# A gated MLP on one core: its three matrix products by one level of Strassen, on fp16 operands, with the layout work moved to DMA

## Chip, core and metric

The kernel runs on one core of a Trainium2 chip; the other cores are idle. The time is that of the device, in microseconds (us), median of several executions. Where stages inside a run are timed, the numbers are those of its one profiled execution. The engines are called PE (matmul; PEld is its weight load), DVE (vector), ACT (scalar), POOL (GpSimd) and SP (sync, which here only issues DMAs). PSUM is the memory that PE adds its results up in; a bank is here one tile of it, 128 x 512 in fp32.

## The reference

```python
# x (8, 1024, 1024), w_gate and w_up (1024, 4096), w_down (4096, 1024), all float32
gate = x @ w_gate
up = x @ w_up
gate = 0.5 * gate * (1 + np.tanh(np.sqrt(2 / np.pi) * (gate + 0.044715 * gate ** 3)))
return ((gate * up) @ w_down).astype(np.float32)
```

There are 8192 tokens. In units of one matmul instruction (128 x 128 stationary, 128 x 512 moving) each of the three products takes 4096, together 12,288.

## The kernel before

It goes through the tokens in 16 passes of 512. In each pass it transposes x on PE, then forms gate and up for 128 columns at a time, then the down product. The casts of the weights to bf16 are made in the first pass by ACT and DVE; gate and up weights are written back in bf16 and read again in each later pass.

```python
for mi in range(n_mt):                       # 16 passes of 512 tokens
    # [cut: load x, cast to bf16]
    for kc in range(KC):
        tp = tpsum_pool.tile([P, MT], BF16, tag="tps")
        for mm in range(MT // P):
            nc.tensor.transpose(tp[:, mm * P:(mm + 1) * P],
                                xbs[mm][:, kc * P:(kc + 1) * P], identity)
        nc.any.tensor_copy(out=xT_sb[:, kc, :], in_=tp)
    for nb in range(n_nb):
        if mi == 0:
            wg_f = wstage_pool.tile([P, KC, NB], FP32, tag="wsf")
            nc.sync.dma_start(out=wg_f, in_=wg_v[:, :, nsl])
            wg_b = wbf_pool.tile([P, KC, NB], BF16, tag="wgb")
            nc.any.tensor_copy(out=wg_b, in_=wg_f)
            nc.sync.dma_start(out=wg_bf[:, :, nsl], in_=wg_b)
            # [cut: the same for w_up]
        else:
            # [cut: load wg_b and wu_b from the bf16 copies]
        for ns in range(n_ns):
            # [cut: pg, pu = PSUM tiles; 8 matmuls into each]
            nc.scalar.activation(gl, pg, mybir.ActivationFunctionType.Gelu_apprx_tanh)
            nc.vector.tensor_tensor(hT_sb[:, ncidx, :], gl, pu, mybir.AluOpType.mult)
    for m128 in range(n_m128):
        for hh in range(n_hh):
            # [cut: po = PSUM tile; 32 matmuls hT_sb x wd_b into it, copy, store]
```

## Time and profile before

| | before |
|---|---|
| time, median | 2801.5 us |
| matmuls of 512 columns | 12,288 |
| PE transposes | 512 |
| one pass of 512 tokens, from the second on | 168.53 us |
| end of the first pass | 268.5 us |

The page of the kernel before, its first two parts: busy time and share by engine, then the granted PE clock, the DMA engines' busy share (both in tenths) and the GB/s in 40 slices of the span.

```profile
...
PE 2720.0 (97%) x12800; PEld 1234.7 (44%) x12800; DVE 395.4 (14%) x583; ACT 536.0 (19%) x803; POOL 0.7 (0%) x6
...
PEclk9899999999999999999999999999999999999999
DMA  9996534525254352534525254351534525244250
GB/s 342 322 288 204 162 99 140 146 92 154 79 159 126 112 154 73 165 104 136 150 91 150 83 158 128 113 150 65 176 106 135 151 71 155 84 123 133 75 154 35
...
```

PE is busy for 97% of the span. The clock is under 90% in the second slice alone (in stretches of 70 us the windows view has 0.90, 0.85, 0.95, and 1.00 from 210 us on); the DMA engines are at 90% or more of their time in the first three slices.

The chain of waits before, in order of time (start, length, what), from its beginning and around two down phases:

```profile
...
2.94 10.78 DMA x_tile<-in_x_dram
...
59.73 9.50 DMA wg_f<-in_w_gate_dram
69.33 1.91 ACT wg_b L103
...
550.35 55.25 PE po L149 x256
718.88 55.25 PE po L149 x256
...
```

The down phase has 256 matmuls in 55.25 us, so one matmul costs 55.25 / 256 = 0.2158 us of the chain. A pass is 718.88 - 550.35 = 168.53 us: 768 matmuls are 165.7, and 2.8 remain for the transposes. In the first pass the chain goes through weight loads of 4 to 11 us and casts of 1.9 instead.

Groups of instructions before (line, engine, operation, tiles, shapes, count, then busy us, mean ns of one, and idle time before):

```profile
...
L149 PE MATMUL po<-wd_b,hT_sb 128*128 128x512 bf16 x4096 | 891.5, 379 | 6.1 <-DVE hT_sb L141 5.7
...
L141 DVE TENSOR_TENSOR hT_sb<-gl,pu 128x512 bf16<-128x512 bf16 x512 | 352.2, 688 | 1473.1 <-PE pu L130 1457.7
...
```

The mean of 379 ns is the latency of one pipelined matmul, not its cost; the cost is the 0.2158 us above. DVE needs 0.69 us to multiply a bank out of PSUM, and is idle for most of the time.

The whole time is thus 12,288 x 0.2158 = 2652, plus 16 x 2.8 = 45 for transposes, plus 100 lost in the first pass, plus 3.6 of tail: 2800.

### The profile page before, as it was taken

The numbers are of one execution on the slowest core, as the hardware profiler recorded it, in microseconds if no ns is written. First come the engines' busy times: TensorE is split into PE (matmuls) and PEld (weight loads), VectorE is DVE, ScalarE is ACT, GpSimd is POOL, SyncE is SP. The second block draws the span as 40 slices with busy tenths as digits, with TensorE's granted clock in tenths as the row PEclk, the third lists the DMA queues.
The fourth block names the chain that finished last, engine by engine and source line by source line (L and its number), as shares of the span: only waits on it lengthen the run. The fifth ranks groups of instructions, "written<-read, shape, count | busy, mean of one in ns | idle before, by whom it ended". The sixth has DMA issues, their size and how long they took to land.

```text
span 2800.1 us, 29616 instructions
## 1 busy us (share of the span) xinstructions
PE 2720.0 (97%) x12800; PEld 1234.7 (44%) x12800; DVE 395.4 (14%) x583; ACT 536.0 (19%) x803; POOL 0.7 (0%) x6
## 2 busy tenths in 40 slices
PE   5779999999999999999999999999999999999999
PEld 2234444444444444444444444444444444444444
DVE  1111101101021120111101011110211101011010
ACT  4442112111121111112111121111112111121110
POOL 0000000000000000000000000000000000000000
PEclk9899999999999999999999999999999999999999
DMA  9996534525254352534525254351534525244250
GB/s 342 322 288 204 162 99 140 146 92 154 79 159 126 112 154 73 165 104 136 150 91 150 83 158 128 113 150 65 176 106 135 151 71 155 84 123 133 75 154 35
DMA packets 597764, 387.82 MB, mean 139 GB/s; under 512 B 11904, under 2 KB 568960, under 8 KB 597632
## 3 DMA queue, kind: packets, MB, share of 16 engines
q1 hardware_dynamic: 597632, 385.92, 44.9%
q8 instruction: 100, 1.64, 0.2%
q14 instruction: 32, 0.26, 0.0%
HBM read 335.54 MB, written 50.33 MB: 138 GB/s over the span
## 4 chain that ended last, share of the span: by engine, by line
PE 92%; DMA 5%; ACT 1%; issue 1%; SPq 0%; DVE 0%; ACTq 0%; DVEq 0%
PE po L149 31%; PE pg L122 30%; PE pu L130 30%; DMA wg_f<-in_w_gate_dram 3%; DMA wu_f<-in_w_up_dram 1%; PE tp L89 1%; ACT wg_b L103 1%; DMA x_tile<-in_x_dram 0%; ACT wu_b L109 0%; SPq L104 0%; DVE xT_sb L94 0%; ACT wd_b L73 0%; SPq L110 0%; SPq L82 0%; DVE wg_b L103 0%
## 5 line engine op out<-in xcount | busy, mean ns | idle before, releaser
L130 PE MATMUL pu<-xT_sb,wu_b 128*128 128x512 bf16 x4096 | 978.8, 382 | 33.3 <-ACT wu_b L109 33.3
L122 PE MATMUL pg<-xT_sb,wg_b 128*128 128x512 bf16 x4096 | 991.1, 382 | 17.8 <-ACT wg_b L103 16.2
L149 PE MATMUL po<-wd_b,hT_sb 128*128 128x512 bf16 x4096 | 891.5, 379 | 6.1 <-DVE hT_sb L141 5.7
L130 PEld LDWEIGHTS <-wu_b 128*128 128x128 bf16 x4096 | 402.1, 98 | 530.8 <-ACT wu_b L109 40.9
L122 PEld LDWEIGHTS <-wg_b 128*128 128x128 bf16 x4096 | 401.8, 98 | 496.5 <-ACT wg_b L103 19.1
L149 PEld LDWEIGHTS <-hT_sb 128*128 128x128 bf16 x4096 | 399.7, 98 | 492.6 <-DVE hT_sb L141 11.7
L138 ACT ACTIVATE gl<-pg 128x512 bf16<-128x512 f32 x512 | 305.7, 597 | 1369.0 <-PE pg L122 1369.0
L141 DVE TENSOR_TENSOR hT_sb<-gl,pu 128x512 bf16<-128x512 bf16 x512 | 352.2, 688 | 1473.1 <-PE pu L130 1457.7
L157 ACT COPY ot<-po 128x512 f32<-128x512 f32 x127 | 74.5, 586 | 819.4 <-PE po L149 813.1
L94 DVE COPY xT_sb<-tp 128x512 bf16<-128x512 bf16 x33 | 13.8, 422 | 811.5 <-PE tp L89 811.5
L89 PE MATMUL tp<-identity,xb_tile 128*128 128x128 bf16 x512 | 48.6, 223 | 19.2 <-DVE xb_tile L84 12.4
L89 PEld LDWEIGHTS <-xb_tile 128*128 128x128 bf16 x512 | 38.0, 99 | 41.5 <-issue 20.8
L94 ACT COPY xT_sb<-tp 128x512 bf16<-128x512 bf16 x95 | 52.1, 588 | 2.2 <-PE tp L89 2.2
L109 ACT CAST wu_b<-wu_f 128x2048 bf16<-128x2048 f32 x16 | 30.3, 1896 | 15.9 <-DMA wu_f<-in_w_up_dram 15.4
L84 ACT CAST xb_tile<-x_tile 128x1024 bf16<-128x1024 f32 x32 | 32.2, 1047 | 6.1 <-DMA x_tile<-in_x_dram 6.1
L103 ACT CAST wg_b<-wg_f 128x2048 bf16<-128x2048 f32 x14 | 26.6, 1898 | 34.9 <-issue 19.0
L84 DVE CAST xb_tile<-x_tile 128x1024 bf16<-128x1024 f32 x32 | 22.1, 690 | 57.9 <-PE tp L89 40.4
L73 ACT CAST wd_b<-wd_f 128x4096 bf16<-128x4096 f32 x5 | 18.0, 3601 | 13.0 <-DMA wd_f<-in_w_down_dram 13.0
L73 DVE CAST wd_b<-wd_f 128x4096 bf16<-128x4096 f32 x3 | 6.9, 2288 | 0.5 <-DMA wd_f<-in_w_down_dram 0.5
L103 DVE CAST wg_b<-wg_f 128x2048 bf16<-128x2048 f32 x2 | 2.4, 1222 | 3.0 <-DMA wg_f<-in_w_gate_dram 3.0
L73 ACT ACT_TABLE_LOAD x1 | 1.3, 1283 | 0.7 <-PEq L176 0.7
L138 ACT ACT_TABLE_LOAD x1 | 1.3, 1283 | 0.0
(7 smaller groups left out, 1.6 us busy)
## 6 DMA issues: line engine op xcount, KB each, us to landing
wg_b<-geglu_wg_bf SPq DMA_DIRECT2D x240, 512.0 KB, 3.9
wu_b<-geglu_wu_bf SPq DMA_DIRECT2D x240, 512.0 KB, 4.5
x_tile<-in_x_dram SPq DMA_DIRECT2D x64, 512.0 KB, 5.6
out_dram<-ot SPq DMA_DIRECT2D x128, 256.0 KB, 2.0
wd_f<-in_w_down_dram SPq DMA_DIRECT2D x8, 2048.0 KB, 9.5
wg_f<-in_w_gate_dram SPq DMA_DIRECT2D x16, 1024.0 KB, 8.4
wu_f<-in_w_up_dram SPq DMA_DIRECT2D x16, 1024.0 KB, 8.3
geglu_wg_bf<-wg_b SPq DMA_DIRECT2D x16, 512.0 KB, 5.5
```

The costliest lines, as they stand in the source:

```text
L73: nc.any.tensor_copy(out=wd_b[:, c * WDC:(c + 1) * WDC, :], in_=wd_f)
L84: nc.any.tensor_copy(out=xb_tile, in_=x_tile)
L89: nc.tensor.transpose(tp[:, mm * P:(mm + 1) * P], xbs[mm][:, kc * P:(kc + 1) * P], identity,)
L94: nc.any.tensor_copy(out=xT_sb[:, kc, :], in_=tp)
L103: nc.any.tensor_copy(out=wg_b, in_=wg_f)
L109: nc.any.tensor_copy(out=wu_b, in_=wu_f)
L122: nc.tensor.matmul(pg, wg_b[:, kc, ns * P:(ns + 1) * P], xT_sb[:, kc, :], start=(kc == 0), stop=(kc == KC - 1),)
L130: nc.tensor.matmul(pu, wu_b[:, kc, ns * P:(ns + 1) * P], xT_sb[:, kc, :], start=(kc == 0), stop=(kc == KC - 1),)
L138: nc.scalar.activation(gl, pg, mybir.ActivationFunctionType.Gelu_apprx_tanh)
L141: nc.vector.tensor_tensor(hT_sb[:, ncidx, :], gl, pu, mybir.AluOpType.mult)
L149: nc.tensor.matmul(po, hT_sb[:, ncidx, m128 * P:(m128 + 1) * P], wd_b[:, ncidx, hh * HT:(hh + 1) * HT], start=(ncidx == 0), stop=(ncidx == ...
L157: nc.any.tensor_copy(out=ot, in_=po)
```

## The change

One level of Strassen (the form with few additions) replaces a 2 x 2 block product's eight half-size products by seven, at the price of sums of blocks. The change does so for gate, up and down. Other parts come with it:

- 8 passes of 1024 tokens, so that each of x's blocks is 512 x 512;
- fp16 for bf16;
- x is cast by a DMA from DRAM to DRAM and transposed by DMA, for the next pass during the current one, and PE transposes nothing;
- weights are cast by DMA while they are loaded. DVE forms their sums. In passes 0, 1 and half of 2 they come from the fp32 source; raw blocks and sums are stored as "operands" in the second half of pass 1 and the first half of pass 2 and loaded from there afterwards;
- the operands of w_down are prepared in pass 0, through one staging tile: load with cast, four sums on DVE, seven stores;
- a product accumulates onto an earlier one in PSUM; ACT copies a bank out before the next product goes on top, DVE adds other banks, POOL multiplies gelu(gate) by up.

The core of the diff (the removed body is the code above; cuts are marked):

```diff
+    def cast_x(p):
+        r = slice(p * TOK, (p + 1) * TOK)
+        nc.gpsimd.dma_start(out=xh[r, :], in_=x2[r, :])
+    def transpose_x(p):
+        for n, kh, mh in (("b11", 0, 0), ("b21", 1, 0), ("b12", 0, 1), ("b22", 1, 1)):
+            r0 = p * TOK + mh * MH
+            nc.sync.dma_start_transpose(
+                out=xq[n], in_=xh[r0 : r0 + MH, kh * MH : (kh + 1) * MH])
+    def sums_x():                      # [cut: t1..t4, four DVE ops of 128 x 2048 fp16]
+    def load_w(p, i):                  # 2 chunks (gate, up) into a ring of 6
+        # [cut]
+            if from_source(p, i):
+                nc.gpsimd.dma_start(out=raw(c), in_=w_v[w][:, :, i * 2 * P : (i + 1) * 2 * P])
+            else:
+                nc.sync.dma_start(out=c, in_=wop[w][i])
+    def from_source(p, i):
+        return p < 2 or (p == 2 and i < NP // 2)
+    def keeps(p, i):
+        return (p == 1 and i >= NP // 2) or (p == 2 and i < NP // 2)
+    def sums_w(p, i, w):               # [cut: four DVE ops of 128 x 512 fp16]
+        if keeps(p, i):
+            nc.sync.dma_start(out=wop[w][i], in_=c)
+    def wd_load(q):                    # one staging tile, in the first half of hq["s3"]
+        st = hq["s3"].rearrange("p a b -> p (a b)")[:, 0:4096]
+        nc.gpsimd.dma_start(out=st.rearrange("p (t h) -> p t h", t=4),
+                            in_=wd_v[:, 4 * q : 4 * q + 4, :])
+    # [cut: wd_sums(k), four DVE ops of 128 x 1024; wd_store(q), seven stores of 256 KB]
+    SEQ = [("P1", 0), ("P1", 1), ("P5", 0), ("P6", 0), ("P6", 1), ("P5", 1), ("P7", 0),
+           ("P7", 1), ("P2", 0), ("P4", 0), ("P4", 1), ("P2", 1), ("P3", 0), ("P3", 1)]
+    # pair(p, i): per entry of SEQ (0 gate, 1 up) four matmuls; banks a, b, c for each of the two:
+    #   P1, P6, P7, P4 accumulate in a; P5, P3 in b; P2 in c
+        def snap(n, w):
+            nc.scalar.activation(tl((n, w)), bank["a", w], COPY, scale=1.0 if w == 0 else HSC)
+        def add(n, b, w):              # w == 1: the same with a scale of 1/16
+            nc.vector.tensor_tensor(o, bank[b, w], o, ADD)
+        def prod(n, h):
+            nc.gpsimd.tensor_tensor(hq[h][:, i, :], t[n, 1], t[n, 0], MUL)
+    # [cut: h21 on DVE; the table that says after which product each of these is issued]
+    # gate_up(p): for i in range(16), with extra work after the k-th product of a pair:
+            extra[1].append(lambda i=i: load_w(p, i + 2) if i + 2 < NP else None)
+            # [cut: if i + 1 < NP:]
+            extra[3].append(lambda i=i: sums_w(p, i + 1, 0))
+            extra[5].append(lambda i=i: sums_w(p, i + 1, 1))
+            if p == 0:                 # every 21 products: load, and 14 to 17 later sums, stores
+                # [cut]
+            if i == 4 and p + 1 < NPASS:
+                extra[2].append(lambda: cast_x(p + 1))
+    # [cut: down(p): 7 products of 2 x 4 x 8 matmuls; x transposes of the next pass at its start]
+    cast_x(0)
+    load_w(0, 0)
+    load_w(0, 1)
+    transpose_x(0)
+    sums_x()
```

A pair is two of the 32 column tiles of gate and up: 14 products of 4 matmuls, 56 matmuls. The up half is scaled by 1/16 on its way out of PSUM, and the output by 16.

## The prediction

> **What bounds the kernel now.** The page: PE busy 2720 of 2800.1 us (97%), chain 92% PE, 5% DMA. In the chain of waits 256 down matmuls take 55.25 us without a gap, so one 128x128x512 matmul costs 0.2158 us (the 379-382 ns of the groups are latency), and a 512-token pass repeats every 168.53 us: 768 matmuls (165.7) plus 2.8 for transposes. The first pass ends at 268.5, 100 us late: there the chain alternates between weight loads (5 to 11 us per MB) and ACT casts (1.9), at clock 0.92 and DMA 0.93 busy (windows view); the GB/s row peaks at 342. 15 passes then run at the matmul rate, clock 1.00.
>
> **What the change removes and adds.**
> 1. PE: 7/8 of 12,288 matmuls is 10,752 of the same shape, no PE transposes; fp16 should stream like bf16. 10,752 x 0.2158 = 2320 us is the floor.
> 2. Per pair (56 matmuls, 12.1 us): DVE six adds and a multiply from PSUM, 7 x 0.69 (trace: hT_sb) = 4.8; eight weight sums of 512 fp16 in passes 0 to 2.5, an estimated 0.42 each (the Trainium skill, "VectorE: DVE Perf Modes", perf-mode tier table: 16-bit tensor_tensor in SBUF runs at 2x, 1224 ns for 2048; no such case in this trace) = 3.4; sums of w_down in pass 0, 1.8. At most 10 of 12.1. ACT: six copies, four gelus at 0.59 = 5.9. Pool: three products plus descriptors of cast DMAs, guessed 6 to 8 (not in this trace). Copies have 1.7 us before their bank is written again. All hidden, if loads are in time.
> 3. DMA: passes 0 to 2.5 read weights from fp32, 2.1 MB a pair. Pass 0 adds 1.4 MB of w_down reads and 1.2 MB of stores: 4.7 MB per 12.1 us, 390 GB/s, above the 342 seen. Pass 0 loses 20 us (0 to 60), passes 1 and 2, which store operands (347 GB/s), 5 to 15. Later passes need 175 GB/s.
> 4. Start: cast of 4 MB x to DRAM, DMA transposes (2 MB; 261 GB/s in the Trainium skill, "DMA: Bandwidth & Descriptors", Latency and other measured facts; unmeasured here), sums: PE starts at 35 to 45 us. Later transposes hide under down.
> 5. Transitions of 16 phases and tail: 10.
>
> **Sum**: 2320 + 40 + 20 + 10 + 10 = 2400, with unforeseen waits **2410 us, 2365 to 2480** (8 in 10). Faster by over 2%: 0.95; within 2%: 0.03; slower: 0.02.
>
> **What would show it.** Step 1: in passes 3 to 7, 56 matmuls take 12.1 us, a pass (1344) 290 us, PE near 100%, clock 1.00. Step 2: DVE under 85%, ACT near 50% in pass 0; hardly any PE wait on ACT copies or DVE adds. Step 3: 330 GB/s or more in the first tenth of the span, PE waits there released by weight sums that wait on loads; pass 0 at 310 to 350 us, passes 1 and 2 at 290 to 305. Step 4: first matmul at 35 to 45 us, after a transpose or x sums.
>
> **What would make it wrong.** Cast DMAs at half the plain rate, or their descriptors filling Pool: passes 0 to 2.5 bind on loads, plus 50 to 150 us. Pool products blocked by DVE sums. DMA transposes over 40 us each pass, holding up DVE behind the x sums. A clock below 1.00 through short gaps. On the low side: pass 0 hidden and a start under 30 us give 2360.

## The result, and the profile after

The median is 2422.2 us (4 runs, 2417.3 to 2424.3), against 2802.6 for the kernel before in the same rounds. The ratio is 0.8642, 95% interval 0.8628 to 0.8655. The median lies in the predicted range, 12 us over the predicted value. Kernels that ran in different sets are best compared by ratios.

The page after, the same lines as before:

```profile
...
PE 2335.6 (96%) x10752; PEld 1055.0 (44%) x10752; DVE 1027.3 (42%) x1504; ACT 830.1 (34%) x1410; POOL 577.8 (24%) x484
...
PEclk8989999999998999999999999999999999999999
DMA  9999666998797465544756455564645645554453
GB/s 152 180 204 211 177 195 97 175 262 272 170 272 239 174 218 194 204 185 174 225 194 206 177 186 193 215 209 176 206 166 221 210 175 187 210 197 174 175 187 109
...
```

PE is at 96% again. The granted clock is under 90% in slices 1, 3 and 13. The DMA engines, at full share in slices 1 to 4 (up to 242 us), move 152 to 211 GB/s there, where before they moved 288 to 342 in the first three.

The chain of waits after: its start, the ends of passes 0 to 2 (the last of the seven down products), and two loads:

```profile
...
1.25 13.50 DMA x_half<-in_x_dram
16.40 13.43 SPq L91
...
44.62 6.18 DMA x_b<-x_half
...
74.11 14.22 DMA h_s<-in_w_down_dram
...
361.00 13.81 PE ps_da L375 x64
...
651.08 13.81 PE ps_da L375 x64
...
728.41 27.61 DMA wc<-in_w_up_dram
...
954.68 13.81 PE ps_da L375 x64
...
```

A down product is 64 matmuls in 13.81 us, which is again 0.2158 each. Line 91 is the DMA transpose; "SPq" is time in which the sync queue issues it. The last down product ends a pass: 361.00 + 13.81 = 374.8, then 664.9 and 968.5; the next ends come 290.1 apart.

Windows after (per stretch: length, then busy us and count by engine, clock, DMA share, GB/s), for the start, a stretch of pass 0's gate and up, and passes 1, 2 and 3:

```profile
...
core 0: us, PE busy (x) PEld busy (x) DVE busy (x) ACT busy (x) POOL busy (x), PEclk, DMA share, GB/s
0.00:54.80 54.80, 3.59 (x9) 1.13 (x10) 5.10 (x6) 2.48 (x3) 6.94 (x12) 0.84 1.15 167
...
150.00:232.00 82.00, 74.41 (x322) 32.49 (x321) 61.88 (x103) 33.19 (x57) 34.22 (x32) 0.94 1.16 211
...
374.80:664.90 290.10, 290.10 (x1346) 131.48 (x1344) 165.81 (x272) 103.70 (x176) 90.74 (x81) 1.00 0.86 196
664.90:968.50 303.60, 293.13 (x1345) 132.25 (x1344) 128.21 (x192) 103.81 (x176) 72.11 (x60) 0.98 0.72 220
968.50:1258.60 290.10, 290.10 (x1345) 131.48 (x1344) 108.03 (x144) 103.50 (x176) 62.39 (x49) 1.00 0.56 196
...
```

Passes 1 and 3 take 290.1 us, which is 1344 x 55.25 / 256 = 290.06: nothing but matmuls, at full clock. The DMA share adds up the times that packets took; over 1 it says that these times overlap on an engine.

POOL's product in the groups after (L261), and the DMA queues (packets, MB, share of 16 engines' span; q1 plain, q0 the casts issued by POOL):

```profile
...
q1 hardware_dynamic: 142208, 400.59, 46.2%
q0 software_dynamic: 88064, 67.12, 19.1%
...
L261 POOL TENSOR_TENSOR h_a<-t 128x512 f16<-128x512 f32 x384 | 496.7, 1294 | 1510.8 <-DVE t L255 1414.5
...
```

The cast queue has 67.12 MB for 19.1% of the span, which is 67.12 MB / (0.191 x 2422.5 us) = 145 GB/s. The listed size is that of the fp16 result (a weight load of 1 MB of fp32 is listed at 512 KB), so 290 GB/s of fp32 are read. The plain queue has 400.59 MB for 46.2%, or 358 GB/s. These are rates per time that packets took, and since packet times overlap, not what the engines can move: from 14 to 18 us the DMA view shows the cast queue alone, with a share of 1.41 and 187 GB/s of result, or 374 of fp32.

```profile
...
DMA packets 1480, 0.75 MB, mean 187 GB/s; under 512 B 17, under 2 KB 1480, under 8 KB 1480
...
q0 software_dynamic: 1480, 0.75, 140.6%
...
```

Counting a cast by its smaller side is the main reason why a full DMA share shows only some 200 GB/s in pass 0.

Who waited for whom after, between 70 and 260 us (total us, times, longest):

```profile
...
DVE h_s L170 <- DMA h_s<-in_w_down_dram: 31.5, 5, 10.9
POOL h_s L153 <- issue: 22.0, 1, 22.0
...
PE ps_a L241 <- ACT t L248: 12.4, 4, 10.8
...
PE ps_b L241 <- DVE t L253: 9.2, 3, 4.1
...
DVE wc L142 <- DMA wc<-in_w_up_dram: 7.0, 3, 3.8
...
```

The tile h_s is the staging tile of w_down. DVE stands before the w_down sums (line 170), POOL before the w_down loads (153), and PE before banks that ACT and DVE have not yet emptied.

The account of the time, from these numbers:

| term | predicted | measured |
|---|---|---|
| 10,752 matmuls x 0.2158 | 2320 | 8 x 290.06 = 2320.5 |
| start: second product at 54.78 instead of 1.73 us | 40 | 53.0 |
| rest of pass 0: 374.8 - 290.1 - 53.0 | 20 | 31.7 |
| pass 1; pass 2 | 5 to 15 together | 0; 303.6 - 290.1 = 13.5 |
| phase changes, and tail | 10 | 0, and 3.6 |
| sum | 2400, given as 2410 | 2422.3, of a span of 2422.5 |

### The profile page after: what moved, and what is told of

The parts are those of the page before. It is cut to its first block, busy times and chain, and to the rows that moved or that the text cites. A ratio compares the mean times of both kernels' runs of the same rounds, so it can differ in the third digit from the quotient of the medians.

```text
span 2422.5 us, 27727 instructions
## 1 busy us (share of the span) xinstructions
PE 2335.6 (96%) x10752; PEld 1055.0 (44%) x10752; DVE 1027.3 (42%) x1504; ACT 830.1 (34%) x1410; POOL 577.8 (24%) x484
## 3 DMA queue, kind: packets, MB, share of 16 engines
q1 hardware_dynamic: 142208, 400.59, 46.2%
q0 software_dynamic: 88064, 67.12, 19.1%
## 4 chain that ended last, share of the span: by engine, by line
PE 90%; DMA 7%; SPq 1%; DVE 1%; issue 0%; POOL 0%; ACT 0%; POOLq 0%; DVEq 0%; ACTq 0%
PE ps_a L241 33%; PE ps_da L375 18%; PE ps_b L241 17%; PE ps_db L375 9%; PE ps_c L241 8%; PE ps_dc L375 5%; DMA h_s<-in_w_down_dram 3%; DMA wd_ops<-h_s 2%; SPq L91 1%; DMA wc<-in_w_up_dram 1%; DMA x_half<-in_x_dram 1%; DMA x_b<-x_half 0%; SPq L189 0%; DVE t L255 0%; DVE h_s L170 0%
## 5 line engine op out<-in xcount | busy, mean ns | idle before, releaser
L241 PEld LDWEIGHTS <-wc 128*128 128x128 f16 x7168 | 704.3, 98 | 940.6 <-issue 63.3
L261 POOL TENSOR_TENSOR h_a<-t 128x512 f16<-128x512 f32 x384 | 496.7, 1294 | 1510.8 <-DVE t L255 1414.5
L241 PE MATMUL ps_a<-x_t,wc 128*128 128x512 f16 x3072 | 728.3, 380 | 12.4 <-ACT t L248 12.4
L248 ACT ACTIVATE t<-ps_a 128x512 f32<-128x512 f32 x768 | 458.0, 597 | 499.1 <-PE ps_a L241 499.1
L375 PEld LDWEIGHTS <-h_a 128*128 128x128 f16 x3072 | 300.6, 98 | 362.5
L375 PE MATMUL ps_da<-dc,h_a 128*128 128x512 f16 x1536 | 335.4, 379 | 0.0
L241 PE MATMUL ps_b<-x_t,wc 128*128 128x512 f16 x1024 | 264.5, 381 | 21.5 <-DVE wc L142 21.5
L241 PE MATMUL ps_a<-x_b,wc 128*128 128x512 f16 x1024 | 246.8, 385 | 29.8 <-DMA x_b<-x_half 29.8
L241 PE MATMUL ps_b<-x_b,wc 128*128 128x512 f16 x1024 | 246.2, 384 | 19.7 <-DVE t L253 19.7
L241 PE MATMUL ps_c<-x_b,wc 128*128 128x512 f16 x1024 | 262.8, 379 | 0.0
L354 DVE TENSOR_TENSOR h_a<-h_a,h_a 128x2048 f16<-128x2048 f16 x96 | 110.2, 1214 | 0.0
L269 ACT ACTIVATE t<-ps_a 128x512 f32<-128x512 f32 x128 | 76.3, 596 | 65.6 <-PE ps_a L241 65.6
L255 DVE SCALAR_TENSOR_TENSOR t<-ps_c,t 128x512 f32<-128x512 f32 x128 | 88.4, 691 | 11.9
```

What stands on the lines that cost most here:

```text
L241: nc.tensor.matmul(ps, lhs(k), rhs[:, k, :], start=(first and k == 0), stop=(k == KH - 1), skip_group_check=True,)
L248: nc.scalar.activation(tl((n, w)), bank["a", w], COPY, scale=1.0 if w == 0 else HSC)
L255: nc.vector.scalar_tensor_tensor(o, bank[b, w], HSC, o, MUL, ADD)
L261: nc.gpsimd.tensor_tensor(hq[h][:, i, :], t[n, 1], t[n, 0], MUL)
L269: nc.scalar.activation(tl("gl21"), bank["a", 0], GELU)
L354: nc.vector.tensor_tensor(hq[o][:, s, :], hq[a][:, s, :], hq[b][:, s, :], op)
```

## The experiments

Each run edits the kernel after, unless it says otherwise. All had three timed rounds.

### Is the gain the matmul count?

`e_eight` issues P3 twice in each pair and each down phase.

```diff
-            for k in range(KH):
+            for k in list(range(KH)) * (2 if name == "P3" else 1):
-                    for n in range(8):
+                    for n in list(range(8)) * (2 if name == "P3" else 1):
```

> The product P3 is issued twice everywhere (wrong result): 12,288 matmuls again, all else as in the kernel after. Theory (the gain is the matmul count): 1536 more matmuls x 0.2158 = 331 us more, so 2754 us, or down to 2720 where longer pairs hide the loads of the first pass better; 0.97 to 0.985 of before, and a steady pass of 1536 x 0.2158 = 331.5 us. Rival (the gain comes from the new pipeline: cast DMAs, DMA transposes, fp16, buffers): 2450 to 2650.

Measured: 2737.3 us, ratio 0.9775 (0.9761 to 0.979); the result is wrong. A steady pass, in the windows view:

```profile
...
1074.00:1405.50 331.50, 331.50 (x1538) 150.29 (x1536) 108.11 (x144) 103.30 (x176) 62.24 (x49) 1.00 0.51 172
...
```

This is 331.5 us, 1536 x 0.2158, and the total lies in the theory's range. So 315 of the 380 us come from doing seven products for eight. Everything else the change does is worth the remaining 65, or 2.3% of the time before. That 315 is not quite 331 has its place too: in this run pass 0 ended at 401.3, which is 70 over a full pass instead of 85, and pass 2 lost 10 instead of 13.5, presumably because a longer pair hides more of the loads.

`e_bf16` changes only the operand type.

```diff
-FP16 = mybir.dt.float16
+FP16 = mybir.dt.bfloat16
```

> The kernel after with bf16 in place of fp16 everywhere. If the operand type does not matter to the matmul rate or to the sums on DVE: 2415 to 2427 us, steady pass 290.0 to 290.1. If fp16 had cost or gained anything per matmul, a steady pass would differ by more than 1 us. The relative error will be several times that of fp16, it may be judged wrong.

Measured: 2421.4 us, ratio 0.8646 (0.8633 to 0.8659), and correct. The time is that of fp16 within the noise, and in the chain a steady pass runs from 964.35 to 1254.43, again 290.1 us.

### The start

The transposes of pass 0 took the chain from 14.8 to 50.8 us. Over all passes a transpose has a median of 5.3 us to landing. The theory: seven cast DMAs (six for three pairs of weights, one for w_down) run beside the first ones. The rival: a transpose is that slow by itself. `e_start` puts five of the seven (all but the first pair) behind the transposes, by a two-element copy on POOL which reads the last of them:

```diff
     cast_x(0)
     load_w(0, 0)
-    load_w(0, 1)
     transpose_x(0)
+    gate = const.tile([P, 2], FP16, name="gate")
+    nc.gpsimd.tensor_copy(out=gate, in_=xq["b22"][:, 0, 0:2])
+    load_w(0, 1)
@@ gate_up: sums of the second pair, in the first pair of pass 0
-                extra[3].append(lambda i=i: sums_w(p, i + 1, 0))
-                extra[5].append(lambda i=i: sums_w(p, i + 1, 1))
+                late = p == 0 and i == 0
+                extra[11 if late else 3].append(lambda i=i: sums_w(p, i + 1, 0))
+                extra[13 if late else 5].append(lambda i=i: sums_w(p, i + 1, 1))
```

> The second weight pair, the third and the first w_down load are issued only after the four transposes of x have landed (a small Pool copy reads the last one), and the first pair's sums for the second come later in program order. Theory A (the first transposes are slow because seven cast DMAs run beside them): they issue at about 2.5 us each as in later passes, the second product (P5) starts at 30 to 38 us instead of 54.8, total 2398 to 2410 if pass 0 gives little back. Theory B (a transpose of freshly cast x takes 8.5 us of the queue by itself): P5 at 48 or later, total 2418 or more.

Measured: 2403.5 us, ratio 0.8584 (0.8571 to 0.8597), correct. The timelines up to 60 us of the sync queue and of PE (start, us it was taken, what), of the kernel after and of this run:

```profile
...
14.76 33.98 SPq L91 DMA_TRANSPOSE x_b<-x_half  x4
...
54.78 1.89 PE L241 MATMUL ps_b<-x_t,wc 128*128 128x512 f16 x4 [21.45 <-DVE wc L142]
...
```

```profile
...
14.60 11.62 SPq L91 DMA_TRANSPOSE x_b<-x_half  x4
...
32.49 1.89 PE L241 MATMUL ps_b<-x_t,wc 128*128 128x512 f16 x4 [6.62 <-DVE wc L142]
...
```

The same four transposes occupy the queue for 11.62 us instead of 33.98. The second product starts at 32.49 us, 22 earlier, and pass 0 ends at 353.1 instead of 374.8, 22 earlier: in the profiled executions all of it is kept (by the ratios the whole run gained 16 us). Both numbers are in theory A's range, and the rival falls. Why it is kept, though DMA time is short later, is not tested; a likely reason: in the kernel after, the loads issued early soon fill the ring, and from 60 to 68 us the windows view shows no DMA at all, where this run has a share of 1.22.

### The rest of pass 0

The waits above suggest theory A: DVE, in order, stands before the w_down sums until the load has landed. `e_sums_free` lets the sums read x instead, with the same DMA traffic.

```diff
     def wd_sums(k):
-        tt, b11, b12, b21, b22 = wd_views()
+        tt = wd_views()[0]
+        b11 = b12 = xq["b11"][:, 0:2, :]
+        b21 = b22 = xq["b12"][:, 0:2, :]
```

> The w_down sums on DVE read x tiles instead of the just loaded w_down tile (wrong result); the loads and stores of w_down stay, so the DMA traffic is the same. Theory A (in pass 0 DVE, which runs in order, stands before the w_down sums until their load has landed, and the PSUM adds behind them come late): the four PE holes between 70 and 232 us go, DVE no longer waits 31 us for w_down, pass 0 ends at 343 to 352 instead of 374.9, total 2390 to 2402. Theory B (the DMA engines are simply full in pass 0): the wait moves to the weight sums, pass 0 ends at 365 or later, total 2412 to 2424.

Measured: 2416.8 us, ratio 0.8634 (0.8621 to 0.8646), result wrong; pass 0 ended at 368.8. Both numbers lie in theory B's range, and theory A fell as the main cause: only 6 us of 32 came back, 1 of them by an earlier start (by the ratios the whole run gained 2 us, within their intervals). Its waits, 70 to 260 us:

```profile
...
POOL h_s L153 <- DMA wd_ops<-h_s: 34.4, 3, 22.0
...
DVE wc L142 <- DMA wc<-in_w_up_dram: 20.1, 8, 4.8
...
DVE wc L142 <- DMA wc<-in_w_gate_dram: 11.9, 6, 4.2
...
```

DVE no longer waits for w_down, but POOL waits 34 us for the staging tile (in the kernel after 5 us of its waits at line 153 were put down to that, and 22 to nothing that the profile shows), and DVE waits 32 us (20.1 + 11.9) for gate and up weights, where it waited 7. This left theory C, order: POOL stands before the next w_down load until the last stores have read the tile, and weight loads behind it on the same engine start late. Or theory B: the DMA engines are full, and the wait goes wherever it can. `e_wd2buf` separates them. It gives w_down a second staging tile and issues each load but the first 14 products earlier; bytes and sums stay.

```diff
-        st = hq["s3"].rearrange("p a b -> p (a b)")[:, 0:4096]
+        st = st2 if q % 2 else hq["s3"].rearrange("p a b -> p (a b)")[:, 0:4096]
-                        (0, lambda q=q: wd_load(q)),
+                        (0 if q == 0 else -14, lambda q=q: wd_load(q)),
```

(The load stands 28 products ahead of the sums where it stood 14.)

> A second staging tile for w_down, each load issued one period earlier; same bytes, same sums, correct. Theory C (in-order waits: Pool stands before a w_down load until the stores of the last one have read the tile, with weight loads and products behind it; DVE stands before sums until the load lands): waits of Pool and DVE on w_down nearly vanish and pass 0 ends at 352 or earlier, total 2400 or less. Theory B (the DMA engines are full from the start to 232 us, whatever waits for what): waits move to the weight loads, pass 0 ends at 362 to 374, total 2410 to 2422.

Measured: 2421.1 us, ratio 0.8643 (0.863 to 0.8656), correct; pass 0 ended at 373.2. The waits of this run in the same stretch:

```profile
...
DVE wc L144 <- DMA wc<-in_w_gate_dram: 19.7, 5, 8.0
DVE wc L144 <- DMA wc<-in_w_up_dram: 15.2, 7, 4.4
...
```

No wait for the staging tile is left in this view, and nothing was gained: 35 us of waits now stand at the weight loads. Within pass 0 two things nearly cancel: the second w_down load was now issued at 14.8 us, beside the transposes, and the second product started at 57.66, 2.9 later; from there pass 0 lost 27.2 us instead of 31.7. So the order of waits was not the main cause, and theory B's forecasts hold, though that the engines are full is not shown by them alone. (The expectation says "one period"; the edit moves the load by 14 of its 21 products.)

`e_nowd` takes the preparation away altogether:

```diff
-            if p == 0:
+            if False:
                 for q in range(8):
@@ load_d
-        nc.sync.dma_start(out=c, in_=wdop[k])
+        nc.sync.dma_start(out=c, in_=xh[0 : 8 * P, 0:HH].rearrange("(a p) h -> p a h", p=P))
```

> No w_down loads, sums or stores in pass 0; the down products read blocks of the cast x instead (wrong result). If the preparation of w_down is the cause of everything that pass 0 loses after its start, pass 0 ends at 343 to 349 (start 53 + 290) and the total is 2388 to 2397. If the cast of the second x or the weight casts alone hold pass 0 up, it ends at 355 or later, total over 2402.

Measured: 2386.2 us, ratio 0.8516 (0.8501 to 0.853), result wrong. The chain of waits has the last product of pass 0 as

```profile
...
322.58 13.81 PE ps_da L377 x64
...
```

so pass 0 ended at 336.4. That and the total lie below the first forecast's ranges: the second product started at 45.81 us, 9 earlier than in the kernel after, which the forecast did not expect. One cast fewer ran beside the transposes, and this fits the other runs: with two casts there the second product came at 32.5 (`e_start`), with seven at 50.3 to 54.8 (six runs), with eight at 57.7 (`e_wd2buf`). From 45.81 on pass 0 took 336.4 - 45.8 = 290.6 for the 1336 matmuls left, which are 288.3: 2.3 us are lost instead of 31.7. So without the preparation of w_down nearly all of the loss is gone. The run takes away the DVE sums along with the traffic; that the sums alone are not the cause rests on `e_sums_free`, which kept them, off their load, and on the next section, where a change of DMA traffic alone takes 12 us off pass 0. The x cast for pass 1 was in pair 4 here too, and without w_down it held up nothing; this points to the sum of the DMA work, and not to one part of it.

An estimate of the DMA work up to 232 us: casts of x (twice 2.1 MB), of 15 pairs of weights (1.05 MB each) and of w_down (8.4 MB) are 28.3 MB of result, at the 187 GB/s of casts alone 151 us; the w_down stores are 14.7 MB, at the plain queue's 358 GB/s 41 us; together 192 us. From 54.8 to 68 us there was no DMA, so 219 us of the stretch were left for it. The engines had work for most of that time, but the estimate does not show them full.

### The cast of the next x, and the operand stores

In pass 2 the chain runs through one weight load of 27.6 us (at 728 us above). Two things stand near it: the 4 MB cast of x in pair 4, ahead of it on POOL's queue, and the operand stores. `e_xcast13` moves the cast to pair 13.

```diff
-            if i == 4 and p + 1 < NPASS:
+            if i == 13 and p + 1 < NPASS:
```

> The cast of the next pass's x is issued in pair 13 instead of pair 4 of each pass, where no weight load follows it on its queue. Theory A (the 4 MB cast holds up the weight loads behind it while operands are stored): pass 2 takes 290 us instead of 303.5, pass 0 gains 5 to 12 as well, total 2397 to 2405; correct. Theory B (the operand stores alone fill the DMA engines in pass 2): a hole stays in the first half of pass 2, total 2416 to 2424.

Measured: 2404.6 us, ratio 0.8593 (0.8578 to 0.8607), correct. Pass 0 ended at 362.4, 12.4 earlier. Pass 2 took 296.9, so only half of its loss went: theory A has the total and the gain of pass 0, but not all of pass 2. Its chain of waits near the wait that remained:

```profile
...
716.02 22.14 DMA wc<-in_w_up_dram
...
```

The load of 22 us is that of pair 7, the last from the source. While it runs, the first loads of stored operands (pair 8) come in as well, and the stores of pairs 6 and 7 are under way. `e_alt` keeps the late cast and spreads the stores:

```diff
-        return p < 2 or (p == 2 and i < NP // 2)
+        return p < 2 or (p == 2 and i % 2 == 0)
-        return (p == 1 and i >= NP // 2) or (p == 2 and i < NP // 2)
+        return (p == 1 and i % 2 == 1) or (p == 2 and i % 2 == 0)
```

> Late x cast as in the run before, and the operand stores of weights alternate (odd pairs in pass 1, even pairs in pass 2) instead of filling pairs 8 to 15 of pass 1 and 0 to 7 of pass 2; correct. Theory (the remaining 6.8 us of pass 2 come from source loads, stores and first reloads meeting around pair 7: about 6.3 MB for one pair): passes 1 and 2 both take 290 to 291.5, total 2396 to 2400. Rival (any stores beside source loads cost time): pass 1 grows to over 292 as well, total 2403 or more.

Measured: 2394.8 us, ratio 0.8551 (0.8538 to 0.8563), correct. Passes 1 and 2:

```profile
...
358.90:649.00 290.10, 290.10 (x1346) 131.52 (x1344) 161.04 (x264) 103.57 (x176) 88.98 (x79) 1.00 0.85 200
649.00:939.10 290.10, 290.10 (x1345) 131.52 (x1344) 134.81 (x200) 103.41 (x176) 73.96 (x62) 1.00 0.75 227
...
```

Both are at the floor of 290.1, as the theory said, with the same bytes and DMA shares of 0.85 and 0.75. Pass 2's loss was two peaks, not a lack of DMA time over the pass.

### Putting it together

`e_best` has the start, the late cast and the alternating stores. It also takes DMA work out of gate and up of pass 0: three of the seven w_down operands are plain blocks, so the first down phase casts them straight from the source and stores them from its own chunks.

```diff
@@ wd_store: (0, b11), (1, b21), (5, b22) left out
@@ load_d
+        v, nb = divmod(k, 2)
+        if p == 0 and v in (0, 1, 5):
+            # [cut: e, hh = which block]
+            nc.gpsimd.dma_start(out=c, in_=src[:, 8 * nb : 8 * nb + 8, e, hh * HH : (hh + 1) * HH])
+            nc.sync.dma_start(out=wdop[k], in_=c)
+        else:
+            nc.sync.dma_start(out=c, in_=wdop[k])
```

> Together: weight loads after the first transposes, late x cast, alternating operand stores, and the three w_down operands that are plain blocks are cast straight from the source for the first down phase and stored from there, not in gate/up of pass 0 (3 of 7 stores moved out of it); correct. If the gains add: 2422 - 22 - 12 - 14 = 2374, and if the DMA engines are what fills pass 0, up to 15 less: 2358 to 2376. If they do not add, because pass 0 is bound by DMA time that only moves: 2380 to 2396.

Measured: 2379.7 us, ratio 0.8495 (0.8483 to 0.8508), correct; between the two forecasts. Gate and up of pass 0 ended at 235 instead of 278 us, but down had a new wait, seen in its chain:

```profile
...
263.78 2.39 SPq L91
...
266.36 6.42 DMA dc<-wd_ops
...
272.92 7.24 PE ps_da L384 x23
```

The third down product started 10 us late, for a load that the sync queue issued at 266.36, behind the block stores (which wait for the casts) and the transposes. `e_best2` took three things at once: stores after the block's matmuls; the x cast behind the first block casts, with the transposes at the third product; and a start with x cast in halves.

```diff
@@ down, after the matmuls of chunk k - 4
                 load_d(p, k)
+                keep_d(p, k - 4)            # the store of the block, if it is one
@@ gate_up: cast_x(p + 1) in the last pair, after the first block casts
@@ down: transpose_x at P6 instead of P1, sums_x at P7 instead of P5
@@ start: x cast as two DMAs of 512 rows; order b11, b12, b22, b21; sums_w before sums_x
```

> The combination once more, with its new 10 us wait taken out: the sync queue no longer issues block stores and transposes ahead of the down loads (stores after the block's matmuls, x cast behind the first block casts, transposes from the third product of down). And a shorter start: x cast in two halves, transposes in the order of use, the first weight sums ahead of the x sums. Correct. Theory (queue order was the cause of that wait): pass 0 of down without a wait over 2 us, P5 at 20 to 27 us, total 2355 to 2371. Rival (pass 0 is bound by its DMA work whatever the order): the time comes back as weight waits, total 2374 or more.

Measured: 2393.4 us, ratio 0.8545 (0.8531 to 0.8559), correct, and worse than `e_best`: the total is in the rival's range. The theory as built failed: the first down phase had PE waits of 6.2 and 12.6 us. The first was for a block cast that took 30 us to land, with the late x cast beside it. The second was for a down load that stood behind the transposes on the sync queue:

```profile
...
276.80 31.77 SPq L91 DMA_TRANSPOSE x_b<-x_half  x4
...
```

They did not wait for the x cast, which was issued at 236.8 and had landed after 37.8 us, at 274.6; they were slow, and as in the start casts (two of blocks) ran beside them. The earlier start (second product at 27.05 us) was partly given back in a wait of 6.7 us at 50 to 56, which came from DVE standing 6.9 us before a w_down sum. `e_best3` is therefore `e_best` with the one step of the store alone:

```diff
@@ against e_best
-            nc.sync.dma_start(out=wdop[k], in_=c)
@@ down
                 load_d(p, k)
+                keep_d(p, k - 4)
```

> The first combination with one change: in the first down phase the three kept blocks are stored after their own matmuls, behind the next down load on the sync queue, instead of right after their cast was issued; x cast, transposes and start as in the first combination; correct. If the 10 us wait before the third down product came from stores that held that queue while they waited for the casts, it goes and the total is 2367 to 2373. If the first down phase is short of DMA time, the wait moves and the total stays at 2376 to 2384.

Measured: 2368.6 us, ratio 0.8457 (0.8443 to 0.8471), correct, and in the first range. The wait is gone:

```profile
...
32.30:235.00 202.70, 196.47 (x886) 87.56 (x887) 150.18 (x272) 92.06 (x158) 94.03 (x86) 0.98 1.08 181
235.00:332.00 97.00, 97.00 (x451) 44.00 (x450) 37.86 (x46) 9.59 (x16) 9.76 (x10) 1.00 1.04 271
...
```

PE is busy for all of the first down phase. This is 2.1% less than the change itself (0.8457 / 0.8642 = 0.9786) and the fastest of all. Of its 2366.6 us in the profile 2320.5 are matmuls; the start costs 31.1, the rest of pass 0 11.3, the tail 3.6.

## Why the prediction was right, point by point

**Step 1, the floor: right.** The steady pass is 290.1 us at clock 1.00, `e_eight` moves it by exactly the matmuls added, and `e_bf16` shows that fp16 costs nothing.

**Step 2, vector work hidden: right.** In gate and up of pass 1 (193 us) DVE was busy 127.1, or 66%, and ACT 94.0, or 49%; PE waited for neither there. In pass 0, for which the shares were predicted, DVE was busy for 153.9 of the 223.3 us from the second product to the down phase, or 69%, and ACT for 93.0, or 42%. There PE did wait 21.6 us for ACT copies and DVE adds, where "hardly any" was predicted; but `e_nowd` has no such wait between its second product and 260 us, so it was not their own work that bound. The Trainium skill ("VectorE: DVE Perf Modes", perf-mode tier table) has 1224 ns for 2048 bf16 elements; the trace agrees for fp16, with a mean of 1214 ns, and the 0.42 us estimated for 512 is what the DVE timeline shows. POOL was guessed at 6 to 8 us a pair; three products at 1.29 us and two load issues at about 0.9 come to 5.7.

**Step 3, DMA-bound in pass 0: right mechanism, two sizes off.** Pass 0 lost 32 us after its start where 20 were given, and with the longer start it ended at 374.8 where "310 to 350" was given. The predicted "330 GB/s or more" was wrong: the row showed about 210 at full share, since casts count their small side (187 GB/s of result are 374 of fp32). And the releaser was predicted to be a weight sum; in the run it was mostly a w_down sum, until `e_wd2buf` moved it to the weights at no change of time. Passes 1 and 2 lost 0 and 13.5 where 5 to 15 were given.

The waits cost more than their length. The Trainium skill ("TensorE: Matmul & The Clock Gate", Part 1) has the clock fall to half after an idle window of about 3.4 us. The PE timeline of the kernel after shows such a fall:

```profile
...
143.89 3.57 PE L241 MATMUL ps_a<-x_t,wc 128*128 128x512 f16 x8 [10.79 <-ACT t L248]
...
```

After 10.79 us idle, the eight matmuls take 3.57 us to their end instead of 1.89, and the windows view has a clock of 0.50 over them. Here a shorter idle time was enough once: after 2.60 us idle before 169.38 the clock was 0.50 from 171 to 173 us, while after 2.54 before 116.54 it stayed at 1.00. Between 70 and 260 us PE waited 21.6 us for banks (the two lines above); most of the other 10 of the 32 are such half-rate stretches: an estimate from the windows view, four stretches after an idle time (54.78 to 60, 143.89 to 151, 169.38 to 174 and 212.28 to 219.5 us), each times what its clock lacked of 1.00, give 8.9.

**Step 4, the start: the term that was mis-sized.** The prediction put "PE starts at 35 to 45 us" and 40 into the sum. PE's first products came at 29.8, but the second product came at 54.8, and the loss was 53. The prediction had taken the transposes at the rate of the Trainium skill ("DMA: Bandwidth & Descriptors", Latency and other measured facts: 261 GB/s), as if alone. They took from 14.8 to 50.8 us for 2.1 MB, 58 GB/s, beside the cast DMAs; `e_start` shows the cause: with two of the seven casts beside them they ended at 28.5, 151 GB/s.

**Step 5, transitions: too high.** Passes 3 to 7 have no loss at all between phases; the tail is 3.6 us. Steps 3 and 4 were together 28 us too low (13.0, 11.7 and 3.5 for pass 2); the 6.4 too many here and the 10 us added for unforeseen waits made up for part of that, and the sum came out 12 us low. That it came out so close is in part luck; that it lies in the range is not, since 2320 of the 2422 us are step 1.

## What to carry to other kernels

When the matmul engine is full, a change in the number of matmuls can be costed to a fraction of a percent from one steady stretch of the chain of waits; what needs judgement is the start, where DMA time was short. There, a wait's name says who ran out first, not what ran out: removing the named wait moved it and left nearly all of the time, while taking away or spreading bytes, and holding back loads that nobody needs yet, shortened it. A queue that issues in order passes one late DMA on to everything behind it, so a store or transpose that must wait belongs behind the loads that need not.

## What the Trainium skill lacked or had wrong

- "DMA: Bandwidth & Descriptors" says which engine must issue a DMA with a cast, but gives no rate for casts. Here weight casts from fp32 to fp16, alone on the DMA engines from 14 to 18 us, moved 187 GB/s of result, or 374 GB/s of source; per time that packets took, all casts of the run moved 145 GB/s of result, and the plain queue 358.
- The same page gives 261 GB/s for DMA transposes, but no rate beside other traffic. Four transposes of 512 KB ran at 58 GB/s beside seven cast loads and at 151 GB/s with five of those held back, and they occupied the issuing queue for 33.98 and 11.62 us.
- No page read says that a profile's DMA bytes for a cast are those of the written side; here a load of 1 MB of fp32 is listed at 512 KB, and in pass 0 a full DMA share shows about 210 GB/s.
